# Decoder layer on one core: fixed order on ScalarE and VectorE through the first block of weights, first granule in quarters, other order of the first transfers

## The chip, the core and the metric

The kernel runs on one core of a Trainium2 chip. The metric is the device time of one execution in microseconds (us). The core has TensorE (PE in the rows; its weight loads are PEld), VectorE (DVE), ScalarE (ACT), GpSimd (POOL) and SyncE (SP, which here only issues transfers), each with an instruction stream of its own that runs in order, and 16 DMA engines. They wait for each other by semaphores.

## What is computed

One decoder layer on 256 tokens of width 2048, all in float32: an RMSNorm, one wide projection into nine parts, an attention branch and a gated MLP branch, and a gated merge.

```
h = rms_norm(x, norm_g)                      # (256, 2048)
q, k, v, z_a, u_b, v_b, z_b, g_a, g_b = split(h @ w_in)
q, k = rms_norm(q, q_norm_g), rms_norm(k, k_norm_g)   # per head
y_a = (attention(q, k, v) * silu(z_a)) @ w_proj_a
sgu = spatial_gating(gelu(u_b), gelu(v_b), sgu_norm_g, w_s, b_s)
y_b = (sgu * silu(z_b)) @ w_proj_b
out = x + (sigmoid(g_a) * y_a + sigmoid(g_b) * y_b) @ w_out
```

The first block of columns, q, is what this case is about: it is multiplied before the norm of x is known, and scaled by it afterwards.

## The kernel before

**Granules.** All weights are read once, as 120 granules of 128 x 2048 float32 (1 MB each). `schedule()` lists them: 8 granules for q, 8 each for k, v, za, vb, ub and zb, then the gates and projections, then the output. A granule `i` of q holds four blocks of 512 columns, of two k tiles (128 rows of the contraction) by two halves of the q columns, in the order 12, 11, 22, 21 (first digit: the k tile; second: the column half).

**Three products.** Every operand is split in two rounded parts: a high half, which ScalarE makes by a cast to fp32r (L120), and a low half, which VectorE makes by subtracting it (L121). `halve` does both, `split(i, pieces)` does it for the weights of granule `i` (`raw` gives `wh` and `wl`), `split_x(kp)` for two k tiles of the transposed x. A product is then three matmuls of 128 x 128 by 512 columns (`three`, L275), so a plain granule takes 24 of them (`direct`). From k on, granules 4, 5, 6 and 7 of a block are plain, and 0 to 3 go by a scheme of seven products (`seven`), for which VectorE makes sums `t` of the weights (L138 to L141) that are split too (`th`, `tl`; the remaining weights are `whp`, `wlp`); such a granule takes 21.

**The first block.** For q the x that is multiplied is not yet normalised. `split_x` multiplies each k tile of x by `norm_g` on ScalarE (L191, 256 columns), casts two of them into `xuh` (L194) and VectorE subtracts to give `xul` (L195). Beside this, `stats` squares the two halves of the plain x (`xnat`, L229), `rsqrt` makes `rstd` of the sums on VectorE and GpSimd (L224, L225), and `stats_row` turns it into a row `R` by two transposes on TensorE (`ps_R`, L235) and a copy. They stand in TensorE's program between the fourth and the fifth granule. From `R` on, `normalise`, `halves_x`, `forms` and `halves_f` make the normalised x for all later blocks (L243, L249, L257 to L260, L267). When q is done it is scaled by `rstd` while it leaves PSUM (L613), and its heads are squared (L339) and scaled (L351).

**What sets the order.** SP issues the transfers in the order of its program: `vec` (the norm vectors, 26 columns), x by k tiles (`load_x`), and the granules (`load`, `load_piece`); a granule's transfer waits for its buffer (four `raw` buffers). On the other engines a scheduler orders instructions when the program is built. Under `tc.manual_schedule` the instructions of ScalarE and VectorE keep among themselves the order in which the code stands; here this covers L581 to L585, the splits of the first four pairs of k tiles and of the first two granules. The loop that follows splits granule `i + 2` and, for `i` under 4, the pair `i + 4` of k tiles, loads granule `i + 3`, and multiplies granule `i`.

Of the kernel before, what the change touches and what calls it, by code (L numbers as in the profile page):

```python
# [64 lines left out]
def hybrid_layer_kernel(  # L65
# [29 lines left out]
    def f(ap):  # L95
        return ap.bitcast(F32)
# [58 lines left out]
    vec = const.tile([P, NVEC], F32, name="vec")  # L155
# [3 lines left out]
    def load_x(p0, p1):  # L159
        nc.sync.dma_start(xt[p0 // 8][:, p0 % 8:(p1 - 1) % 8 + 1, :],  # L160
                          xT[:, NVEC + p0 * S:NVEC + p1 * S].rearrange("p (k t) -> p k t", t=S))

    new_raw(0)
    nc.sync.dma_start(vec, xT[:, 0:NVEC])
    load_x(0, 2)
    load_piece(0, 0, 512)
    load_piece(0, 512, 1024)
    load_x(2, 4)
    load_piece(0, 1024, WORDS)
    load_x(4, 8)  # L170
    load(1, pieces=2)
    load_x(8, 12)
    load(2, pieces=2)
# [14 lines left out]
    def split_x(kp):  # L188
        i, a = kp // 4, 2 * (kp % 4)
        for j in range(2):  # L190
            nc.scalar.activation(xt[i][:, a + j, :], xt[i][:, a + j, :], AF.Copy,  # L191
                                 scale=vec[:, 2 * kp + j:2 * kp + j + 1])
        src = xt[i][:, a:a + 2, :]
        nc.scalar.copy(xu_h[i][:, a:a + 2, :], src)  # L194
        nc.vector.tensor_tensor(xu_l[i][:, a:a + 2, :], src, f(xu_h[i][:, a:a + 2, :]), op=ALU.subtract)  # L195
# [23 lines left out]
    R = const.tile([P, S], F32, name="R")  # L219
# [59 lines left out]
    def direct(L, hs, ls, i, kp, start, stop):  # L279

        t, a = kp // 4, 2 * (kp % 4)
        for c in range(4):
            r, col = c // 2, c % 2
            for kh in range(2):
                hi = hs[t][:, a + kh, r * P:(r + 1) * P]
                lo = ls[t][:, a + kh, r * P:(r + 1) * P]
                o = BLK[f"{kh + 1}{col + 1}"] * B
                three(L[c], hi, lo, wh[i][:, o:o + B], wl[i][:, o:o + B], start and kh == 0, stop and kh == 1,
                      first=(i == 0))
# [291 lines left out]
    with tc.manual_schedule(engines={mybir.EngineType.Activation, mybir.EngineType.DVE}):  # L581
        for kp in range(4):
            split_x(kp)
            if kp < 2:
                split(kp, 2)  # L585
    E, L = [0, 2, 4, 3], [1, 5, 6, 7]
    e = None
    for i, (kind, name, c, kp, n) in enumerate(G):
        if i < 4:
            split_x(i + 4)  # L590
        load(i + 3, pieces=2 if i < 2 else 1)
        split(i + 2)
# [116 lines left out]
```

## Time and profile before

| | |
|---|---|
| median of three runs | 692.8 us (692.78 to 693.59) |
| profiled execution | 692.96 us |
| its span, first to last instruction | 691.2 us |
| TensorE busy | 664.2 us (96%), 3018 matmuls |
| VectorE busy | 553.6 us (80%) |
| ScalarE busy | 388.9 us (56%) |
| DMA | 135.31 MB, mean 196 GB/s |

The share of busy time is a mean over stages that differ, so it doesn't tell by itself what a change is worth. A row of the timeline has the start, the duration, the engine, the line in the code, the operation, what it writes and reads by the names of the program, the number of instructions in the row, and, in brackets, how long the engine was idle ahead of it and what ended that wait. Matmuls overlap: the distance between two starts is what one costs, not the duration. All times are counted from the start of the span.

### The profile page before, as it was taken

How to read it: one execution, taken by the hardware profiler on the slowest of the kernel's cores; microseconds unless marked ns; L12 is line 12 of the kernel's file. 1: busy time of each engine (PE TensorE's matmuls, PEld its weight loads, DVE VectorE, ACT ScalarE, POOL GpSimd, SP SyncE). 2: the span in 40 equal slices, each digit the busy share in tenths (PEclk: the TensorE clock that was granted, in tenths of full speed). 3: DMA queues.
4: the chain of work that ended last, by engine and by line, in shares of the span. 5: the costliest groups of instructions: out<-in, count | busy, mean ns of one | idle time of the engine just before them, and what ended most of it. 6: DMA issues, size and time to landing. Idle time of an engine off the chain costs nothing.

```text
span 691.2 us, 7699 instructions
## 1 busy us (share of the span) xinstructions
PE 664.2 (96%) x3018; PEld 547.6 (79%) x3018; DVE 553.6 (80%) x498; ACT 388.9 (56%) x453; POOL 37.0 (5%) x28
## 2 busy tenths in 40 slices
PE   2799999999999999999999999999999999999997
PEld 0588778888889888788877888888888888888886
DVE  0669789989999899999898998878968886754451
ACT  2959757955785477564745744563554455333330
POOL 1000400500000006200000000000000000000000
PEclk9999999999999999999999999999999999999999
DMA  8863436563274454525734834854563576856610
GB/s 315 332 212 119 167 128 252 183 241 132 116 300 166 162 195 146 228 114 183 290 136 167 320 122 183 303 183 156 220 245 142 201 263 213 267 189 227 235 47 30
DMA packets 22211, 135.31 MB, mean 196 GB/s; under 512 B 2592, under 2 KB 2976, under 8 KB 7200
## 3 DMA queue, kind: packets, MB, share of 16 engines
q1 hardware_dynamic: 21024, 132.73, 51.9%
q10 hardware_dynamic: 1152, 2.10, 1.1%
q8 instruction: 23, 0.38, 0.2%
q14 instruction: 12, 0.10, 0.0%
HBM read 132.72 MB, written 2.10 MB: 195 GB/s over the span
## 4 chain that ended last, share of the span: by engine, by line
PE 85%; DVE 8%; DMA 2%; issue 2%; ACT 2%; POOL 1%; SPq 0%; DVEq 0%; ACTq 0%
PE acc_g L275 14%; PE y L275 13%; PE acc_out L275 13%; PE seven_g L275 5%; PE acc_ub L275 4%; PE acc_v L275 4%; PE acc_q L275 4%; PE acc_za L275 4%; PE acc_vb L275 4%; PE acc_zb L275 4%; DMA xt<-in_xT 2%; PE acc_k L275 2%; DVE wl L121 2%; PE seven_v L275 2%; PE seven_ub L275 2%
## 5 line engine op out<-in xcount | busy, mean ns | idle before, releaser
L121 DVE TENSOR_TENSOR wl<-raw,wh 128x2048 fp32r<-128x2048 f32 (+1 forms) x82 | 182.7, 2236 | 65.6 <-ACT wh L120 65.3
L120 ACT CAST wh<-raw 128x2048 fp32r<-128x2048 f32 (+1 forms) x82 | 153.0, 1870 | 106.5 <-PE acc_out L275 42.2
L120 ACT CAST th<-t 128x2048 fp32r<-128x2048 f32 x40 | 76.5, 1912 | 105.6 <-DVE t L141 105.5
L121 DVE TENSOR_TENSOR tl<-t,th 128x2048 fp32r<-128x2048 f32 x40 | 92.0, 2301 | 28.2 <-ACT th L120 27.6
L275 PE MATMUL acc_out<-wh,mT 128*128 128x512 f32 x256 | 79.0, 390 | 0.0
L120 ACT CAST whp<-raw 128x1536 fp32r<-128x1536 f32 x40 | 59.1, 1480 | 34.5 <-DMA raw<-in_w 16.2
L121 DVE TENSOR_TENSOR wlp<-raw,whp 128x1536 fp32r<-128x1536 f32 x40 | 70.1, 1752 | 0.0
L275 PEld LDWEIGHTS acc_out<-wh,mT 128*128 128x128 f32 x256 | 47.9, 188 | 9.9
L275 PE MATMUL acc_g<-wh,xh 128*128 128x512 f32 x128 | 49.8, 389 | 0.0
L275 PE MATMUL acc_out<-wl,mT 128*128 128x512 f32 x128 | 49.8, 389 | 0.0
L275 PE MATMUL acc_g<-wh,xl 128*128 128x512 f32 x128 | 49.7, 389 | 0.0
L138 DVE TENSOR_TENSOR t<-raw 128x1024 f32<-128x1024 f32 x40 | 48.8, 1221 | 0.6
L275 PE MATMUL acc_g<-wl,xh 128*128 128x512 f32 x128 | 48.8, 389 | 0.0
L275 PE MATMUL acc_q<-wh,xuh 128*128 128x512 f32 x64 | 26.0, 407 | 16.9 <-ACT wh L120 16.9
L225 POOL TENSOR_TENSOR rs<-ms,mhalf 128x4 f32<-128x4 f32 x12 | 29.8, 2506 | 126.0 <-DVE ms L224 126.0
L275 PEld LDWEIGHTS acc_q<-wh,xuh 128*128 128x128 f32 x64 | 12.6, 196 | 20.2 <-ACT wh L120 17.8
L275 PEld LDWEIGHTS acc_g<-wl,xh 128*128 128x128 f32 x128 | 24.0, 188 | 5.2
L275 PEld LDWEIGHTS acc_g<-wh,xl 128*128 128x128 f32 x128 | 24.0, 188 | 5.1
L140 DVE TENSOR_TENSOR t<-t,raw 128x512 f32<-128x512 f32 x40 | 27.8, 694 | 0.3
L275 PEld LDWEIGHTS acc_out<-wl,mT 128*128 128x128 f32 x128 | 24.0, 188 | 4.9
L275 PEld LDWEIGHTS acc_g<-wh,xh 128*128 128x128 f32 x128 | 24.0, 188 | 4.9
L141 DVE TENSOR_TENSOR t<-t,raw 128x512 f32<-128x512 f32 x40 | 27.4, 686 | 0.3
(452 smaller groups left out, 1447.4 us busy)
## 6 DMA issues: line engine op xcount, KB each, us to landing
raw<-in_w SPq DMA_DIRECT2D x115, 1024.0 KB, 4.9
raw<-in_w SPq DMA_DIRECT2D x9, 512.0 KB, 8.6
xnat<-in_x SPq DMA_DIRECT2D x2, 1024.0 KB, 12.0
xres<-in_x ACTq DMA_DIRECT2D x8, 256.0 KB, 5.3
out<-xres SPq DMA_DIRECT2D x7, 256.0 KB, 4.5
xt<-in_xT SPq DMA_DIRECT2D x3, 512.0 KB, 9.2
xt<-in_xT SPq DMA_DIRECT2D x2, 256.0 KB, 4.1
raw<-in_w SPq DMA_DIRECT2D x2, 256.0 KB, 5.4
```

The lines of the kernel that those rows point to most:

```text
L120: nc.scalar.copy(h, r)
L121: nc.vector.tensor_tensor(l, r, f(h), op=ALU.subtract)
L138: nc.vector.tensor_tensor(two, r[:, B:3 * B].rearrange("p (a n) -> p a n", a=2), r[:, None, 0:B].to_broadcast([P, 2, B]), op=ALU.add)
L140: nc.vector.tensor_tensor(t[:, 2 * B:3 * B], t[:, 0:B], r[:, 2 * B:3 * B], op=ALU.add)
L141: nc.vector.tensor_tensor(t[:, 3 * B:], t[:, 2 * B:3 * B], r[:, 3 * B:], op=ALU.add)
L225: nc.gpsimd.tensor_tensor(dst, ms[:, :n], mhalf[:, :n], op=ALU.pow)
L275: nc.tensor.matmul(acc, a, b, start=(start and n == 0), stop=(stop and n == 2))
```

## The change

The tile `vec` becomes `xv`, which also takes the first k tile of x; its first transfer brings both. The first granule comes in pieces of 512, 512 and 1024 columns, the second k tile between them, and the other transfers at the start alternate in another order: `raw3` is issued whole ahead of the last piece of x and of `xnat`, and `raw4` whole behind them. `R` takes the place of the first k tile in `xv`. `split_x` can take one k tile alone, and the first granule is split by quarters, each beside the k tile that it is multiplied with; the second granule is split in quarters too, the third in halves. `direct` multiplies the first granule quarter by quarter. The manual order of ScalarE and VectorE goes on through the loop until the eighth granule, and in the loop the split of the weights stands ahead of that of x.

```diff
--- before.py
+++ after.py
@@ -152,7 +152,9 @@
         return ap.rearrange("p (h d) -> p h d", d=P)
 
 
-    vec = const.tile([P, NVEC], F32, name="vec")
+
+    xv = const.tile([P, NVEC + S], F32, name="xv")
+    vec = xv[:, 0:NVEC]
     xt = [slot(F32, f"xt{i}").rearrange("p (k t) -> p k t", t=S) for i in range(2)]
     xu_h, xu_l = [], []
 
@@ -161,16 +163,17 @@
                           xT[:, NVEC + p0 * S:NVEC + p1 * S].rearrange("p (k t) -> p k t", t=S))
 
     new_raw(0)
-    nc.sync.dma_start(vec, xT[:, 0:NVEC])
-    load_x(0, 2)
-    load_piece(0, 0, 512)
-    load_piece(0, 512, 1024)
+    nc.sync.dma_start(xv, xT[:, 0:NVEC + S])
+    load_piece(0, 0, B)
+    load_piece(0, B, 2 * B)
+    load_x(1, 2)
+    load_piece(0, 2 * B, WORDS)
     load_x(2, 4)
-    load_piece(0, 1024, WORDS)
+    load(1, pieces=2)
     load_x(4, 8)
-    load(1, pieces=2)
+    load(2, pieces=2)
     load_x(8, 12)
-    load(2, pieces=2)
+    load(3)
     load_x(12, 16)
     xn = [slot(F32, f"xnat{m}") for m in range(2)]
     for m in range(2):
@@ -185,14 +188,15 @@
     for _ in range(8):
         nc.tensor.matmul(ps_w, warm[:, 0:P], warm, start=True, stop=True)
 
-    def split_x(kp):
+    def split_x(kp, js=None):
         i, a = kp // 4, 2 * (kp % 4)
-        for j in range(2):
-            nc.scalar.activation(xt[i][:, a + j, :], xt[i][:, a + j, :], AF.Copy,
-                                 scale=vec[:, 2 * kp + j:2 * kp + j + 1])
-        src = xt[i][:, a:a + 2, :]
-        nc.scalar.copy(xu_h[i][:, a:a + 2, :], src)
-        nc.vector.tensor_tensor(xu_l[i][:, a:a + 2, :], src, f(xu_h[i][:, a:a + 2, :]), op=ALU.subtract)
+        for j in js or range(2):
+            src = xv[:, NVEC:] if kp + j == 0 else xt[i][:, a + j, :]
+            nc.scalar.activation(xt[i][:, a + j, :], src, AF.Copy, scale=vec[:, 2 * kp + j:2 * kp + j + 1])
+        sl = slice(a + js[0], a + js[0] + 1) if js else slice(a, a + 2)
+        src = xt[i][:, sl, :]
+        nc.scalar.copy(xu_h[i][:, sl, :], src)
+        nc.vector.tensor_tensor(xu_l[i][:, sl, :], src, f(xu_h[i][:, sl, :]), op=ALU.subtract)
 
     ident = const.tile([P, P], F32, name="ident")
     make_identity(nc, ident)
@@ -216,7 +220,7 @@
         nc.sync.dma_start(gain, bass.AP(tensor=sg.tensor, offset=sg.offset, ap=[[0, P], [1, P]]))
 
     rstd = const.tile([P, 2], F32, name="rstd")
-    R = const.tile([P, S], F32, name="R")
+    R = xv[:, NVEC:]
     ssum = const.tile([P, 2], F32, name="ssum")
 
     def rsqrt(dst, src, n, count):
@@ -279,14 +283,16 @@
     def direct(L, hs, ls, i, kp, start, stop):
 
         t, a = kp // 4, 2 * (kp % 4)
-        for c in range(4):
+        order = [(c, kh) for c in range(4) for kh in range(2)]
+        if i == 0:
+            order = [(c, kh) for kh in range(2) for col in (1, 0) for c in (col, 2 + col)]
+        for c, kh in order:
             r, col = c // 2, c % 2
-            for kh in range(2):
-                hi = hs[t][:, a + kh, r * P:(r + 1) * P]
-                lo = ls[t][:, a + kh, r * P:(r + 1) * P]
-                o = BLK[f"{kh + 1}{col + 1}"] * B
-                three(L[c], hi, lo, wh[i][:, o:o + B], wl[i][:, o:o + B], start and kh == 0, stop and kh == 1,
-                      first=(i == 0))
+            hi = hs[t][:, a + kh, r * P:(r + 1) * P]
+            lo = ls[t][:, a + kh, r * P:(r + 1) * P]
+            o = BLK[f"{kh + 1}{col + 1}"] * B
+            three(L[c], hi, lo, wh[i][:, o:o + B], wl[i][:, o:o + B], start and kh == 0, stop and kh == 1,
+                  first=(i == 0))
 
     def seven(E, L, i, kp, first, last, started):
 
@@ -578,18 +584,28 @@
     for c in range(4):
         at(first["out", 0] + 4 * c - 2, load_res, c)
 
-    with tc.manual_schedule(engines={mybir.EngineType.Activation, mybir.EngineType.DVE}):
-        for kp in range(4):
-            split_x(kp)
-            if kp < 2:
-                split(kp, 2)
+    ordered = ExitStack()
+    ordered.enter_context(tc.manual_schedule(engines={mybir.EngineType.Activation, mybir.EngineType.DVE}))
+    split_x(0, [0])
+    split(0, 4, [0])
+    split(0, 4, [1])
+    split_x(0, [1])
+    split(0, 4, [2])
+    split(0, 4, [3])
+    for kp in range(1, 4):
+        split_x(kp)
+        if kp < 2:
+            split(kp, 4)
     E, L = [0, 2, 4, 3], [1, 5, 6, 7]
     e = None
     for i, (kind, name, c, kp, n) in enumerate(G):
+        if i == 8:
+            ordered.close()
+        if i:
+            load(i + 3)
+        split(i + 2, 2 if i == 0 else 1)
         if i < 4:
             split_x(i + 4)
-        load(i + 3, pieces=2 if i < 2 else 1)
-        split(i + 2)
         plain = i < 8
         if kind == "quad":
             if n == 0:
```

The sequence of ScalarE at its start; `xt0` and `xt1` hold the k tiles 0 to 7 and 8 to 15 of x, `wh0` is the high half of the first granule. Before:

```order
L191 ACT_TABLE_LOAD
L191 ACTIVATE xt0_74<-xt0_74,vec_73 128x256 x2
L191 ACTIVATE xt1_75<-xt1_75,vec_73 128x256 x8
L194 CAST xuh0_96<-xt0_74 128x512
L120 CAST wh0_133<-raw0_76 128x1024 x2
L191 ACTIVATE xt0_74<-xt0_74,vec_73 128x256 x2
L194 CAST xuh1_98<-xt1_75 128x512
L194 CAST xuh0_96<-xt0_74 128x512
L120 CAST wh1_143<-raw1_84 128x1024 x2
```

After:

```order
L195 ACT_TABLE_LOAD
L195 ACTIVATE xt0_74<-xv_73 128x256
L198 CAST xuh0_98<-xt0_74 128x256
L120 CAST wh0_133<-raw0_76 128x512 x2
L195 ACTIVATE xt0_74<-xt0_74,xv_73 128x256
L198 CAST xuh0_98<-xt0_74 128x256
L120 CAST wh0_133<-raw0_76 128x512 x2
L195 ACTIVATE xt0_74<-xt0_74,xv_73 128x256 x2
L198 CAST xuh0_98<-xt0_74 128x512
L120 CAST wh1_150<-raw1_83 128x512 x4
```

The eight scalings of `xt1` have gone from in front of the first casts, and the first cast of weights stands behind one scaling and one cast; each of the first pieces is half as large.

The sequence of ScalarE around the squares of `xnat` (L229, then L233), on which `rstd` waits. Before:

```order
L120 CAST wh3_204<-raw3_162 128x2048
L194 CAST xuh1_98<-xt1_75 128x512
L229 ACTIVATE xnat0_92,ssum_126<-xnat0_92 128x2048
L120 CAST wh4_238<-raw4_201 128x2048
L229 ACTIVATE xnat1_93,ssum_126<-xnat1_93 128x2048
L194 CAST xuh1_98<-xt1_75 128x512
L120 CAST wh5_277<-raw5_236 128x2048
L120 CAST wh6_311<-raw6_275 128x2048
```

After:

```order
L120 CAST wh3_208<-raw3_91 128x2048
L195 ACTIVATE xt1_75<-xt1_75,xv_73 128x256 x2
L198 CAST xuh1_100<-xt1_75 128x512
L120 CAST wh4_242<-raw4_206 128x2048
L195 ACTIVATE xt1_75<-xt1_75,xv_73 128x256 x2
L198 CAST xuh1_100<-xt1_75 128x512
L233 ACTIVATE xnat0_94,ssum_127<-xnat0_94 128x2048
L233 ACTIVATE xnat1_95,ssum_127<-xnat1_95 128x2048
L120 CAST wh5_281<-raw5_240 128x2048
L195 ACTIVATE xt1_75<-xt1_75,xv_73 128x256 x2
```

Before, the first square stood ahead of `wh4`; now both stand behind it and behind the sixth and seventh pair of k tiles.

The sequence of TensorE in the third and fourth granule of k's block (`th10`, `tl10`, `th11`, `tl11` are the split sums of these two, `Fh` a form of x). Before:

```order
L275 MATMUL acc_k0_0_470<-whp11_504,xl0_411 128x512
L275 MATMUL acc_k0_0_470<-whp11_504,xh0_410 128x512
L275 MATMUL acc_k0_0_470<-wlp11_505,xh0_410 128x512
L275 MATMUL acc_k0_1_471<-whp11_504,Fl_415 128x512
L275 MATMUL acc_k0_1_471<-whp11_504,Fh_414 128x512
L275 MATMUL acc_k0_1_471<-wlp11_505,Fh_414 128x512
L275 MATMUL acc_k0_2_472<-th11_508,xl0_411 128x512
L275 MATMUL acc_k0_2_472<-th11_508,xh0_410 128x512
L275 MATMUL acc_k0_2_472<-tl11_509,xh0_410 128x512
L275 MATMUL seven_k0_0_582<-whp11_504,xl0_411 128x512
```

After:

```order
L279 MATMUL acc_k0_2_481<-tl10_476,xh0_418 128x512
L279 MATMUL seven_k0_1_592<-tl10_476,Fh_422 128x512
L279 MATMUL seven_k0_2_593<-tl10_476,Fh_422 128x512
L279 MATMUL seven_k0_3_594<-tl10_476,Fh_422 128x512
L279 MATMUL acc_k0_2_481<-th11_517,xl0_419 128x512
L279 MATMUL acc_k0_2_481<-th11_517,xh0_418 128x512
L279 MATMUL seven_k0_1_592<-th11_517,Fl_423 128x512
L279 MATMUL seven_k0_1_592<-th11_517,Fh_422 128x512
L279 MATMUL seven_k0_2_593<-th11_517,Fl_423 128x512
L279 MATMUL seven_k0_2_593<-th11_517,Fh_422 128x512
L279 MATMUL acc_k0_2_481<-tl11_518,xh0_418 128x512
```

The row with `tl11` was the ninth of the fourth granule and the 78th of the block; now the products of the third granule with `tl10` and six with `th11` stand ahead of it, and it is the 85th.

## Rows read from the trace of the kernel before

**Rows 1.** The page's slices: TensorE's busy tenths in 40 equal slices of the span.

```profile
PE   2799999999999999999999999999999999999997
```

**Rows 2.** Timeline of ScalarE, start of the span: start, duration, what, [idle before <-releaser].

```profile
14.72 1.70 ACT L191 ACTIVATE xt<-xt,vec 128x256 f32<-128x256 f32 x4 [8.60 <-DMA xt<-in_xT]
18.55 1.70 ACT L191 ACTIVATE xt<-xt,vec 128x256 f32<-128x256 f32 x4 [2.13 <-DMA xt<-in_xT]
...
20.67 1.99 ACT L120 CAST wh<-raw 128x1024 fp32r<-128x1024 f32 x2
...
27.11 1.90 ACT L120 CAST wh<-raw 128x2048 fp32r<-128x2048 f32 x1
28.91 0.61 ACT L194 CAST xuh<-xt 128x512 fp32r<-128x512 f32 x1
```

**Rows 3.** Timeline of TensorE, the block of q.

```profile
21.76 0.80 PE L275 MATMUL acc_q<-wh,xuh 128*128 128x512 f32 x1 [16.92 <-ACT wh L120]
...
26.17 0.63 PE L275 MATMUL acc_q<-wh,xuh 128*128 128x512 f32 x1
26.60 0.52 PE L275 MATMUL acc_q<-wh,xul 128*128 128x512 f32 x1
...
46.24 0.38 PE L235 MATMUL ps_R<-ident,rstd 128*128 128x128 f32 x2
```

**Rows 4.** DMA issues of the first 2 us: KB each, median us to landing.

```profile
xt<-in_xT SPq DMA_DIRECT2D x1, 256.0 KB, 2.6
...
vec<-in_xT SPq DMA_DIRECT2D x1, 13.0 KB, 1.9
```

**Rows 5.** Timeline of GpSimd, the powers that make the norms.

```profile
39.89 1.21 POOL L225 TENSOR_TENSOR rstd<-ms,mhalf 128x2 f32<-128x2 f32 x1 [36.78 <-DVE ms L224]
76.31 6.93 POOL L225 TENSOR_TENSOR rs<-ms,mhalf 128x4 f32<-128x4 f32 x4 [35.20 <-DVE ms L224]
```

**Rows 6.** Window 10 to 12 us: busy by engine, clock, DMA share, GB/s (last).

```profile
10.00:12.00 2.00, 0.00 (x0) 0.00 (x0) 0.00 (x0) 0.00 (x0) 0.00 (x0) 1.00 1.03 420
```

**Rows 7.** Timeline of ScalarE, the first square and the reading of its sum.

```profile
33.60 1.91 ACT L229 ACTIVATE xnat<-xnat 128x2048 f32<-128x2048 f32 x1
35.42 0.18 ACT L229 ACTIVATION_READ_ACCUMULATOR xnat<-xnat 128x1 f32 x1
```

**Rows 8.** Windows behind two waits of TensorE: third column from the end is PEclk.

```profile
89.00:90.00 1.00, 1.00 (x4) 0.81 (x3) 1.00 (x2) 1.00 (x5) 0.00 (x0) 0.50 0.00 0
360.00:365.00 5.00, 5.00 (x23) 4.02 (x23) 5.00 (x3) 4.36 (x3) 0.00 (x0) 1.00 0.51 210
```

**Rows 9.** Timeline of TensorE, a wait in the block of the gates.

```profile
359.73 0.50 PE L275 MATMUL acc_g<-th,xl 128*128 128x512 f32 x1 [1.72 <-ACT th L120]
```

**Rows 10.** Timeline of TensorE, the block of k.

```profile
68.23 0.39 PE L275 MATMUL acc_k<-wh,xl 128*128 128x512 f32 x1
...
87.65 0.50 PE L275 MATMUL acc_k<-tl,xh 128*128 128x512 f32 x1 [1.59 <-DVE tl L121]
...
92.33 0.40 PE L275 MATMUL acc_k<-wh,xl 128*128 128x512 f32 x1
```

**Rows 11.** Timeline of VectorE, from the normalisation to the sums of k.

```profile
50.36 4.49 DVE L243 TENSOR_TENSOR xt<-xt,R 128x2048 f32<-128x2048 f32 x2
54.77 2.29 DVE L121 TENSOR_TENSOR wl<-raw,wh 128x2048 fp32r<-128x2048 f32 x1
...
59.17 0.69 DVE L257 TENSOR_TENSOR F<-xt 128x512 f32<-128x512 f32 x1
...
70.39 1.22 DVE L138 TENSOR_TENSOR t<-raw 128x1024 f32<-128x1024 f32 x1
71.52 1.75 DVE L121 TENSOR_TENSOR wlp<-raw,whp 128x1536 fp32r<-128x1536 f32 x1
```

**Rows 12.** Timeline of ScalarE, eviction of q and the last of its squares.

```profile
66.78 2.42 ACT L613 ACTIVATE q<-acc_q,rstd 128x512 f32<-128x512 f32 x4
...
73.66 0.20 ACT L339 ACTIVATION_READ_ACCUMULATOR junk<-q 128x1 f32 x1
```


## The prediction

> **What bounds the kernel now.** I read the page's slices first. The row of TensorE is full from the second slice to the last but one [rows 1]: apart from its first 20 us, TensorE sets the end, and a gain has to come from TensorE starting earlier or waiting less. Second, the timeline of ScalarE shows what keeps it from starting. After the first two k tiles ScalarE takes two groups of four scalings of `xt` that wait 8.60 us and 2.13 us for transfers; by the order of the program they belong to `xt1`, that is to the fifth to eighth granule. Only behind them come `xuh0` and the cast of `wh0` at 20.67 [rows 2]. Third, the timeline of TensorE: the first matmul of the block of q starts at 21.76 after a wait of 16.92 us for that cast [rows 3].
>
> **The start itself.** With the new order ScalarE needs, ahead of the first matmul, the transfer `xv`, one scaling, one cast of 256 columns and one of 512. `xv` is issued first; the nearest rows are `vec` (13 KB, 1.9 us) and the first `xt` (256 KB, 2.6 us) [rows 4], so it lands some 2.7 to 3.4 us into the span, and the first quarter of the weights two to four us later. A scaling is 0.43 (four in 1.70), a cast of 512 columns 0.61 [rows 2]; a cast of 256 isn't in the trace, it lies between nothing and that 0.61, and I take 0.35, since it would be nearer to the scaling of the same size. The first matmul then starts between 4 and 10; I take 7, some 14.8 us earlier. **This isn't the gain**, since TensorE soon meets something that moved less.
>
> **The cap: the transposes `ps_R` in front of the fifth granule.** They stand in TensorE's order ahead of its matmuls and need `rstd`, which needs the squares of both `xnat`. Before, `rstd` was there at 41.1 (39.89 + 1.21) [rows 5], and TensorE came to `ps_R` only at 46.24 [rows 3]. After, ScalarE's order there is the cast of `wh4`, scalings and cast of `xt1`, square, square, and `raw4` stands behind both `xnat` on the queue of SP. The DMA engines are the clock: they move 420 GB/s [rows 6]. At 18.55 a scaling was let go by the last piece of `xT` [rows 2]; up to that piece the queue held 5.26 MB (`vec` 13 KB, `xT` 2.10, three granules of 1.05). After, up to the end of `raw4`, it holds `xv` and the rest of `xT` 2.11 MB, five granules 5.24, `xnat` 2.10, `gain` 0.07: 9.52 MB. The other 4.26 MB take 10.1 us, so `raw4` lands at **28.7**. ScalarE is idle by then: up to `raw3` it is 5.78 MB, so 19.8, and the cast of it and one more split of x end 3.2 later. From 28.7: cast `wh4` 1.8 (27.11 to 28.91), two scalings and a cast 1.35 [rows 2], two squares of 1.9 (33.60 to the next instruction behind 35.42) [rows 7], `ms` with its hops, which I put at 0.25, GpSimd 1.21 [rows 5]. That is 28.7 + 1.8 + 1.35 + 3.8 + 0.25 + 1.2 = **37.1**. TensorE is there first: the 96 matmuls from 46.24 to 68.23 take 0.23 each [rows 3, 10], at the low clock 0.43 (26.17 to 26.60) [rows 3]; one granule of 24 at 0.43 is 10.3, three at 0.23 are 16.5, so from 7 it has done four at 33.8. A start 3 us later than I take costs nothing. `ps_R` moves from 46.24 to 37.1: **-9.1 us**.
>
> **What the wait costs behind it.** In the trace of before, after its long wait, TensorE starts a matmul every 0.43 us until 26.60: eleven from 21.76 in 4.84 us [rows 3], where 0.23 each would be 2.5. [...] Here it idles some 3.3 us ahead of `ps_R`, and I charge the same: **+2.3 us**. [...]
>
> **Where the block of k gains.** Before, this block begins at 68.23, and its 78th matmul, the first with `tl11`, starts at 87.65 [rows 10]. 77 at 0.23 are 17.6 us, so 1.8 were lost. The next 13 take until 92.33, 4.7 us where 3.0 would do: 1.7 more at the low clock. `th11` stood behind scalings of q, which waited for GpSimd. After, one scaling stands ahead of `th10`, three ahead of `th11`, and TensorE takes the first product with `tl11` in the 85th place. Does VectorE keep up? The block of q ends at T = 37.1 + 22.0 + 2.3 = 61.4. VectorE's chain starts with `R`: ScalarE has a cast `wh5` (1.8) and the last split of x (1.35) behind the squares, then the copy `R`, about 0.4, and `wh6` 1.8, so `wl6` starts at 41.0. From there to the end of `t11`: seven subtractions of 2.2 (2.29, overlapping by 0.08), two normalisations 4.4, two `wlp` of 1.7, four forms of 0.6, two sums t of 2.3 (1.13 + 2 x 0.6), `ms` 0.5, a wait of 1.9 for `xh1`: 15.4 + 4.4 + 3.4 + 2.4 + 4.6 + 0.5 + 1.9 = 32.6, so 73.6 [rows 11]. On ScalarE, q is evicted and squared in 7.1 us (66.78 to 73.86) [rows 12], to 68.5; `ms` is at 70.4 on VectorE, GpSimd adds 0.25 + 1.73 (6.93 / 4) [rows 5], one scaling 0.3, `th10` 1.8 to 74.5, three scalings 0.9, `th11` 1.8 to 77.2, `tl11` 2.2 to 79.4. TensorE wants it at T + 84 x 0.23 = 80.7, 1.3 us later. So the loss goes: **-3.5 us**.
>
> **What costs nothing.** Quarters in the first two granules are four more casts on ScalarE and four more subtractions on VectorE. Two casts of 1024 columns take 1.99 [rows 2], four of 512 some 2.1 to 2.4: 0.1 to 0.4 a granule, ahead of ScalarE's idle time from 23.0 to 28.7, which hides it; without that cover it would be up to 0.8. [...] `R` in the place of the first k tile orders its copy behind the scalings, which are on the same engine. `raw3` and `raw4` in one transfer instead of two change no byte count.
>
> **Sum.** -9.1 + 2.3 - 3.5 = -10.3 us. The profiled execution took 692.96 us (span 691.2), the median is 692.8; 692.96 - 10.3 = 682.7, against the median 682.5. I forecast **682.6 us**.
>
> **The rivals.** (1) *VectorE takes over.* Its margin at `tl11` is 1.3 us, since its normalisation moves from 50.36 [rows 11] to 43.2, 7 us, and TensorE 10. If `R` or `th11` is 2 us late, the stall of before stays, 682.6 + 3.5 = 686.1, and two such give 689.6. For it: in those rows VectorE goes from one instruction to the next without idle time. Against: the new order of TensorE puts its products later. Chance 0.24. (2) *The clock stays up behind `ps_R`, or `raw4` lands earlier*: 682.6 - 2.3 = 680.3, with both 679. For it the wait at 359.73, against it those at 21.76 and 87.65. 0.13. (3) *Slower than before*: TensorE, now 3 us nearer to VectorE, waits for `tl` in granule after granule of k, v and za, each time with the low clock behind it. One such wait costs 3.5, as at 87.65; it decides from the third on (682.6 + 3 x 3.5 = 693.1), and with four the time is 696.6. Against: each wait of TensorE lets VectorE get ahead, so the second is less likely than the first. 0.05. (4) *It doesn't do what it says*: the first pieces land no sooner and the front still starts near 20. Then `ps_R` is 24.5 us behind it as before, near 44.5: 1.7 us, and at most the 3.5 of k, 687.6 to 692.8. ScalarE's order is fixed in the program, so only the transfers could do it, and the new order puts the needed ones first. 0.04.
>
> **How the numbers follow.** My own case has 0.54, between 680.8 and 685 (`raw4` an us off, half the slow stretch). The range, 679.0 to 688.5, takes in rival 2 and the first stall of rival 1 and leaves out the rest. A measurement of this kernel tells about 0.2%, 1.4 us, from no change. Faster by more: 0.54 + 0.24 + 0.13 and a part of rival 4, 0.92; within it 0.03; slower 0.05.
>
> **What would show it.** Right: the first matmul between 4 and 10; ScalarE idle ahead of `wh4`, which starts near 28.7; TensorE idle ahead of `ps_R`, which starts near 37; matmuls 0.43 apart behind it; the block of k beginning near 61.4; no wait for `tl11`. Wrong: TensorE still in its fourth granule at 37, `ps_R` before 35 or after 39, or waits for `tl` or `wl` behind 61.

## The result, and the profile after

The changed kernel takes **687.2 us** (median; runs from 687.0 to 687.55) against 692.9 for the kernel before on the same chip: a ratio of 0.992, 95% interval 0.9908 to 0.9933. It is faster, by 5.7 us (0.8%, clear of the noise) where 10.3 were forecast; 687.2 lies in the range of 679.0 to 688.5, in its upper quarter, and outside the 680.8 to 685 of the prediction's own case. The profiled execution took 687.05, with a span of 685.3.

The page's slices are read first again, against [rows 1]: TensorE's busy tenths.

```profile
PE   8789999999999999999989999999999999999997
```

The empty first slice is gone; there is a dent in the third, and that is the wait ahead of `ps_R`. The timeline of ScalarE answers to [rows 2] (start, duration, what, [idle before <-releaser]):

```profile
3.07 0.51 ACT L195 ACTIVATE xt<-xv 128x256 f32<-128x256 f32 x1 [0.99 <-DMA xv<-in_xT]
...
28.36 1.91 ACT L120 CAST wh<-raw 128x2048 fp32r<-128x2048 f32 x1 [5.58 <-DMA raw<-in_w]
...
38.67 0.37 ACT L240 COPY xv<-ps_R 128x256 f32<-128x256 f32 x1
```

The copy of `R` (the last row) stood at 48.02 in the kernel before:

```profile
48.02 0.36 ACT L236 COPY R<-ps_R 128x256 f32<-128x256 f32 x1
```

GpSimd makes `rstd` in 0.71 us, where [rows 5] had 1.21:

```profile
35.81 0.71 POOL L229 TENSOR_TENSOR rstd<-ms,mhalf 128x2 f32<-128x2 f32 x1 [32.71 <-DVE ms L228]
```

And the timeline of TensorE answers to [rows 3] and [rows 10]: first matmul, `ps_R`, the first matmuls of the blocks of k, v and g.

```profile
6.46 0.50 PE L279 MATMUL acc_q<-wh,xuh 128*128 128x512 f32 x1 [1.61 <-ACT wh L120]
...
36.57 0.69 PE L239 MATMUL ps_R<-ident,rstd 128*128 128x128 f32 x2 [6.82 <-POOL rstd L229]
36.91 0.78 PE L279 MATMUL acc_q<-wh,xul 128*128 128x512 f32 x1
...
39.60 0.40 PE L279 MATMUL acc_q<-wh,xul 128*128 128x512 f32 x1
...
60.04 0.39 PE L279 MATMUL acc_k<-wh,xl 128*128 128x512 f32 x1
...
102.41 0.39 PE L279 MATMUL acc_v<-wh,xl 128*128 128x512 f32 x1
...
334.52 0.39 PE L279 MATMUL acc_g<-wh,xl 128*128 128x512 f32 x1
```

Set beside the kernel before, the blocks start earlier by:

| block | before | after | earlier by | length before | length after |
|---|---|---|---|---|---|
| `ps_R` | 46.2 | 36.6 | 9.7 | | |
| k | 68.2 | 60.0 | 8.2 | 44.5 | 42.4 |
| v | 112.8 | 102.4 | 10.4 | 42.8 | 45.3 |
| za | 155.6 | 147.7 | 7.9 | 48.0 | 48.0 |
| vb | 203.6 | 195.7 | 7.9 | 48.8 | 48.9 |
| ub | 252.4 | 244.6 | 7.8 | 43.3 | 44.8 |
| zb | 295.7 | 289.4 | 6.3 | 44.5 | 45.1 |
| g | 340.2 | 334.5 | 5.7 | | |

So the forecast gain was there: 10.4 us at the start of v, by the working 10.3. **4.7 us of it were given back behind that point**: 2.5 in v, 0.1 in vb, 1.5 in ub, 0.6 in zb (they are called the 4.6 us below: 10.3 forecast less 5.7 measured). From g on the two kernels run alike. The waits view of TensorE in the changed kernel says by what (us in total, times, longest):

```profile
PE ps_R L239 <- POOL rstd L229: 6.8, 1, 6.8
PE acc_g L279 <- ACT th L120: 3.1, 2, 1.7
...
PE acc_v L279 <- ACT th L120: 1.3, 2, 0.7
...
PE acc_ub L279 <- ACT th L120: 0.8, 1, 0.8
PE acc_k L279 <- ACT th L120: 0.8, 1, 0.8
PE acc_ub L279 <- DVE tl L121: 0.7, 1, 0.7
PE acc_zb L279 <- ACT th L120: 0.3, 1, 0.3
```

The waits in g stand in the kernel before too [rows 9]. The other rows below the first are short waits for `th` and `tl`, the halves of the sums in the scheme of seven products. In v, ub and zb the kernel before had none.

### The profile page after: what moved, and what is told of

It is laid out like the page before. It is cut to its first block, busy times and chain, and to the rows that moved or that the text cites. A ratio compares the mean times of both kernels' runs of the same rounds, so it can differ in the third digit from the quotient of the medians.

```text
span 685.3 us, 7695 instructions
## 1 busy us (share of the span) xinstructions
PE 664.1 (97%) x3018; PEld 545.4 (80%) x3018; DVE 554.3 (81%) x504; ACT 390.4 (57%) x459; POOL 31.9 (5%) x28
## 4 chain that ended last, share of the span: by engine, by line
PE 69%; DVE 15%; issue 5%; ACT 4%; DMA 4%; SPq 1%; POOL 0%; DVEq 0%; ACTq 0%
PE acc_g L279 14%; PE y L279 13%; PE acc_out L279 13%; PE seven_g L279 5%; PE acc_za L279 4%; PE acc_vb L279 4%; DMA raw<-in_w 4%; DVE wl L121 3%; ACT th L120 2%; PE acc_zb L279 2%; DVE wlp L121 2%; PE acc_v L279 2%; DVE t L138 2%; DVE tl L121 2%; PE acc_ub L279 2%
## 5 line engine op out<-in xcount | busy, mean ns | idle before, releaser
L121 DVE TENSOR_TENSOR wl<-raw,wh 128x2048 fp32r<-128x2048 f32 (+2 forms) x87 | 183.2, 2116 | 68.0 <-ACT wh L120 67.8
L120 ACT CAST wh<-raw 128x2048 fp32r<-128x2048 f32 (+2 forms) x87 | 153.7, 1774 | 103.8 <-PE acc_out L279 45.7
L279 PEld LDWEIGHTS acc_out<-wh,mT 128*128 128x128 f32 x256 | 47.9, 188 | 9.8
L279 PE MATMUL acc_g<-wl,xh 128*128 128x512 f32 x128 | 48.8, 389 | 0.0
L229 POOL TENSOR_TENSOR rs<-ms,mhalf 128x4 f32<-128x4 f32 x12 | 25.2, 2119 | 128.4 <-DVE ms L228 128.4
L279 PE MATMUL acc_q<-wl,xuh 128*128 128x512 f32 x64 | 25.7, 401 | 0.3 <-DVE wl L121 0.2
```

The costliest lines, as they stand in the source:

```text
L120: nc.scalar.copy(h, r)
L121: nc.vector.tensor_tensor(l, r, f(h), op=ALU.subtract)
L229: nc.gpsimd.tensor_tensor(dst, ms[:, :n], mhalf[:, :n], op=ALU.pow)
L279: nc.tensor.matmul(acc, a, b, start=(start and n == 0), stop=(stop and n == 2))
```

## The experiments

Three theories were set against each other for the 4.6 us. **A**: VectorE's whole work from `R` on paces the kernel, so the end follows the start of that chain. **B**: the places that the scheduler gave ScalarE's casts in v (a scaling of k that waits for GpSimd stands ahead of a cast `th`). **C**, formed after the first four runs: VectorE's work inside v to ub is too long for what TensorE leaves it, and what is saved before v doesn't count. Beside these, the parts of the change were tried one by one. All ratios are to the kernel before. "Third" or "fourth granule" of a block means its place in the order of multiplication (4, 5, 0, 1, 6, 2, 3, 7).

### What the start needs: parts of the change alone

**The fixed order alone**, in the kernel before:

```diff
-    with tc.manual_schedule(engines={mybir.EngineType.Activation, mybir.EngineType.DVE}):
-        for kp in range(4):
+    ordered = ExitStack()
+    ordered.enter_context(tc.manual_schedule(engines={mybir.EngineType.Activation, mybir.EngineType.DVE}))
+    for kp in range(4):
...
-        if i < 4:
-            split_x(i + 4)
+        if i == 8:
+            ordered.close()
         load(i + 3, pieces=2 if i < 2 else 1)
         split(i + 2)
+        if i < 4:
+            split_x(i + 4)
```

> The kernel before, its transfers and halves left as they are, with the fixed order on ScalarE and VectorE carried on through the block of q alone. The first matmul then waits for two k tiles and half a granule and starts some 3 us later than the 6.46 of the changed kernel. If the start has slack because ps_R waits for rstd (6.8 us of wait in the changed kernel), ps_R comes within 1 us of 36.6 and the time is 687.2, within 0.9 of the changed kernel. If the new transfers and quarters carry part of the gain, ps_R comes 3 us later or more and the time is 690 or above.

Measured: 688.37 us, ratio 0.9931 (0.9917 to 0.9946). The first matmul starts at 8.69, and the wait ahead of `ps_R` is 1.91 in place of 6.82:

```profile
37.62 0.43 PE L235 MATMUL ps_R<-ident,rstd 128*128 128x128 f32 x2 [1.91 <-POOL rstd L225]
```

The order alone brings 4.6 of the 5.7 us. Whether the other 1.2 us belong to the change isn't shown: the two intervals overlap, and `ps_R`, 1.05 later here, moves as much between kernels that are alike up to it (36.57 in the changed kernel, 37.71 in the run with the scaling behind the cast below). The next run tries the halves by themselves.

**Halves in place of quarters**, in the changed kernel:

```diff
-        if i == 0:
-            order = [(c, kh) for kh in range(2) for col in (1, 0) for c in (col, 2 + col)]
...
-    split_x(0, [0])
-    split(0, 4, [0])
...
-            split(kp, 4)
+    for kp in range(4):
+        split_x(kp)
+        if kp < 2:
+            split(kp, 2)
...
-        split(i + 2, 2 if i == 0 else 1)
+        split(i + 2)
```

> The changed kernel with the first two granules in halves again and the first granule's products in the old order; transfers and the fixed order as in the changed kernel. If the start has slack ahead of ps_R: the first matmul 1 to 3 us later than 6.46, ps_R within 1 us of 36.6 and the same time, 687.2. If the quarters carry gain: 688.5 or more.

Measured: 687.15, ratio 0.992 (0.9903 to 0.9937), against 687.2 with quarters. The first matmul is 2.5 us later, and the wait ahead of `ps_R` takes it up:

```profile
8.94 0.80 PE L279 MATMUL acc_q<-wh,xuh 128*128 128x512 f32 x1 [4.09 <-ACT wh L120]
...
36.61 0.69 PE L239 MATMUL ps_R<-ident,rstd 128*128 128x128 f32 x2 [3.77 <-POOL rstd L229]
```

The quarters and the new order of products are worth nothing that can be measured. What the fixed order alone lacks belongs to the transfers, if to a part of the change at all; that wasn't tried by itself.

**Without the fixed order**, the new transfers and quarters alone (the order ended ahead of the loop over the granules):

```diff
     E, L = [0, 2, 4, 3], [1, 5, 6, 7]
+    ordered.close()
...
-        if i == 8:
-            ordered.close()
```

> The changed kernel with the fixed order ended behind the first two granules, as in the kernel before: new transfers and quarters alone. The scheduler then puts eight scalings of xt1 ahead of the first cast again; the last of them needs the last piece of xT, which now stands behind 6.3 MB in place of 5.26, 2.5 us later. If the fixed order is what frees TensorE's start: the first matmul near 24, ps_R near 48 and a time between 692 and 695. If transfers and quarters carry the gain: ps_R near 37 and 687 to 688.

Measured: 693.51, ratio 1.001 (1.0001 to 1.002). ScalarE's timeline has the eight scalings back ahead of the first cast. The second four of them wait for a transfer until 20.31, and TensorE starts behind them (a row of each engine):

```profile
20.31 1.70 ACT L195 ACTIVATE xt<-xt,xv 128x256 f32<-128x256 f32 x4 [2.06 <-DMA xt<-in_xT]
```

```profile
22.88 0.79 PE L279 MATMUL acc_q<-wh,xuh 128*128 128x512 f32 x1 [18.03 <-ACT wh L120]
```

The fixed order is what frees the start. (`ps_R` came at 46.1, not at 48: TensorE made its four granules in 23.2 us where [rows 3] had 24.5.)

### What holds TensorE ahead of `ps_R`

**The squares one granule earlier**, into the 5.58 us in which ScalarE waits for `raw4`:

```diff
-    at(i0 + 2, stats)
+    at(i0 + 1, stats)
```

> The changed kernel with the two squares for rstd put one granule earlier in ScalarE's order, ahead of the cast of wh4, into ScalarE's idle time of 5.6 us that waits for raw4. rstd then comes near 30 in place of 36.5, ps_R waits little or nothing (TensorE's fourth granule ends near 29.8), and the copy R comes near 35 in place of 38.67, since the cast wh5 and a split of x stay ahead of it. Theory A, the end follows the chain that starts at R: 3.6 us less, 683.6. If TensorE's wait at ps_R is what counts: 6 to 7 us less, 680.5. If waits in v and ub absorb an earlier start: 687.2.

Measured: **683.56**, ratio 0.9865 (0.985 to 0.9879), the 683.6 of theory A, and 3.6 us better than the changed kernel. ScalarE's and TensorE's timelines:

```profile
35.14 0.37 ACT L240 COPY xv<-ps_R 128x256 f32<-128x256 f32 x1
```

```profile
29.27 0.38 PE L239 MATMUL ps_R<-ident,rstd 128*128 128x128 f32 x2
30.27 0.50 PE L279 MATMUL acc_q<-wh,xul 128*128 128x512 f32 x1 [0.61 <-ACT wh L120]
...
32.60 0.53 PE L279 MATMUL acc_q<-wl,xuh 128*128 128x512 f32 x1 [1.59 <-DVE wl L121]
```

So the cap of the prediction is shown: with `rstd` earlier, `ps_R` starts 7.3 us earlier and waits for nothing. Of the 7.3, 4.4 arrive at the block of k (55.6), since now `wh4` and `wl4`, which need `raw4`, are late, with slow matmuls behind (0.43 apart from 33.35 to 35.91). The waits in v, ub and zb are all still there (v lasts 44.9, ub 44.7, zb 45.4): moving everything forward by some 4 us doesn't change what is lost behind v. `R` is copied 3.5 us earlier (35.14 against 38.67), v starts 3.5 us earlier and the end comes 3.6 us earlier: that is theory A's forecast.

### Where the 4.6 us went

**2.2 us less for VectorE ahead of v**: the subtraction for one half of `xl` is left out, in the block of q (lines of the edit that only keep the tile apart are not shown).

```diff
         nc.scalar.copy(xh[i], xt[i])
+        if i == 1:
+            xl[i] = xu_l[i]
+            return
         nc.vector.tensor_tensor(xl[i], xt[i], f(xh[i]), op=ALU.subtract)
```

> The changed kernel without the subtraction that forms the low half of the second eight normalised k tiles (2.2 us of VectorE right behind the first normalisation; the low half of the unscaled tiles stands in its place), the order of everything else on ScalarE and VectorE unchanged. Theory A, VectorE's work from R on sets the end: 2.2 us less, 685.0. If TensorE's own chain or waits for ScalarE set it: no change, 687.2.

Measured: 687.61, ratio 0.992 (0.9903 to 0.9936): nothing gained. In this profile v starts at 102.3 and lasts 45.3, with the same three waits, at the same places within 0.2 us. That takes nothing from theory A, because the time of this subtraction wasn't on the chain. VectorE's timeline in the changed kernel, and then without it:

```profile
47.35 2.29 DVE L253 TENSOR_TENSOR xl<-xt,xh 128x2048 fp32r<-128x2048 f32 x1 [1.98 <-ACT xh L252]
49.56 2.29 DVE L121 TENSOR_TENSOR wl<-raw,wh 128x2048 fp32r<-128x2048 f32 x1
```

```profile
49.47 2.29 DVE L121 TENSOR_TENSOR wl<-raw,wh 128x2048 fp32r<-128x2048 f32 x1 [3.78 <-ACT wh L120]
```

VectorE's next instruction waits for ScalarE's cast `wh` and starts where it did before, so the 2.2 us became idle time. What does set the start of v shows when the copy of `R` is taken as zero (all in us; the last three columns are distances):

| kernel | copy of `R` | start of v | `R` to k | `R` to v | `R` to g |
|---|---|---|---|---|---|
| before | 48.0 | 112.8 | 20.2 | 64.7 | 292.1 |
| new transfers, without the fixed order | 47.9 | 111.4 | 20.2 | 63.5 | 292.0 |
| changed | 38.7 | 102.4 | 21.4 | 63.7 | 295.8 |
| fixed order alone | 39.7 | 103.5 | 20.0 | 63.8 | 295.7 |
| early squares | 35.1 | 98.9 | 20.5 | 63.7 | 295.7 |
| early squares, normalisation split (below) | 36.2 | 99.9 | 18.4 | 63.7 | 295.7 |
| subtraction left out (this run) | 39.0 | 102.3 | 22.1 | 63.3 | 295.4 |

In all twelve traces with the fixed order, v starts 63.3 to 63.8 us behind the copy of `R`, while the block of k starts anywhere from 18.4 to 22.7 behind it; the waits of TensorE in k take up the difference. So up to v the chain of ScalarE and VectorE that goes through this copy paces the kernel, as theory A has it, and a TensorE that reaches k sooner gains nothing.

**2.2 us less for VectorE in v**: one subtraction `wl` left out, ahead of the final sums of k. In the changed kernel it starts at 101.91, half a us ahead of v.

```diff
+                if i != first["v", 0] + 1:
+                    wl[i] = wpool.tile([P, WORDS], F32R, tag="wl", bufs=3, name=f"wl{i}")
+            if i == first["v", 0] + 1:
+                nc.scalar.copy(wh[i], r)
+                wl[i] = wh[i]
+                return
```

> The changed kernel without one subtraction wl (2.2 us of VectorE just ahead of the final sums of k; the granule of v that uses it takes the high half in place of the low one); the order through the block of v is otherwise unchanged. Theory C, VectorE's list between the start of v and its second cast th is too long: the block of v takes 43.5 or less in place of 45.3, with no or one wait in place of three; what follows then waits in ub as before, so 685.5. Theory B, the scaling that waits for GpSimd or the release of a buffer by TensorE makes these waits: 45.3 and 687.2.

Measured: 684.97, ratio 0.9897 (0.9881 to 0.9914): 2.2 us less than the changed kernel, as much as VectorE was spared. The windows view by block, VectorE alone (window, its length, busy us and instructions, PEclk, DMA share, GB/s), shows where: v and the sum of the four blocks v, za, vb, ub, of the kernel before and of the changed one, and v, ub and the sum of this one.

```profile
112.80:155.60 42.80, 40.25 (x38) 1.00 0.54 197
...
sum 182.90, DVE 174.41; mean DVE 43.60
```

```profile
102.40:147.70 45.30, 39.88 (x37) 1.00 0.51 187
...
sum 187.00, DVE 174.72; mean DVE 43.68
```

```profile
102.50:146.60 44.10, 38.60 (x36) 1.00 0.53 196
...
243.40:286.80 43.40, 42.49 (x54) 1.00 0.48 183
sum 184.30, DVE 172.49; mean DVE 43.12
```

From the start of v to the end of ub VectorE works the same 174 us before and after, but the stretch has grown from 182.9 to 187.0. VectorE's idle time grew from 8.5 to 12.3 us, most of it in v (from 2.6 to 5.4). Take 2.2 us of its work out at the start of v, and the stretch shrinks by 2.7: v by 1.2, and ub by 1.4, a hundred microseconds on, where both waits are gone.

In v VectorE's instructions keep their order, and its rows stand some 2.3 us earlier (the `tl` of v's fourth granule at 119.86, not 122.16): there its work is on the path, which theories A and C both have. The gain in ub can't be put down to the work alone. The scheduler chose another order in this kernel, which the expectation took to be as before at least through v: on ScalarE in v, za and vb, on VectorE in za, vb and ub. In ub VectorE now makes the `ms` of vb's norms ahead of the sums they stood behind, and no longer waits 0.98 us for GpSimd, as in the changed kernel (first row), but 0.16 (second):

```profile
261.90 1.93 DVE L365 SCALAR_TENSOR_TENSOR vb_c<-vb_c,rs,gain 128x128 f32<-128x128 f32 x7 [0.98 <-POOL rs L229]
```

```profile
259.04 2.19 DVE L370 SCALAR_TENSOR_TENSOR vb_c<-vb_c,rs,gain 128x128 f32<-128x128 f32 x8 [0.16 <-POOL rs L234]
```

So theory C isn't separated from an order of instructions that suits ub better.

**The scaling of k behind the cast `th`** (theory B by itself: nothing else changes place on ScalarE and VectorE). In the changed kernel the idle time of VectorE in v lies at two places, shown here by the rows of ScalarE and VectorE. The second stands in the kernel before too (2.05 us, at 145.41); at the first it had 0.39 (at 128.40). The cast at 137.36 is put down to TensorE, but the sum `t` of VectorE that it casts ends only 0.11 us ahead of it.

```profile
119.64 0.70 ACT L357 ACTIVATE k_c<-k_c,rs 128x128 f32<-128x128 f32 x2 [3.43 <-POOL rs L229]
120.24 1.89 ACT L120 CAST th<-t 128x2048 fp32r<-128x2048 f32 x1
...
137.36 1.91 ACT L120 CAST th<-t 128x2048 fp32r<-128x2048 f32 x1 [4.62 <-PE seven_v L279]
```

```profile
122.16 2.29 DVE L121 TENSOR_TENSOR tl<-t,th 128x2048 fp32r<-128x2048 f32 x1 [3.27 <-ACT th L120]
...
139.30 2.29 DVE L121 TENSOR_TENSOR tl<-t,th 128x2048 fp32r<-128x2048 f32 x1 [2.05 <-ACT th L120]
```

```diff
+            if fn is norm_qk and a[0] == "k":
+                with tc.issue_after(getattr(cast_t[i + 0], "ins", cast_t[i + 0])):
+                    fn(*a)
```

(`cast_t[i]` is ScalarE's cast `th` of v's fourth granule; the lines that keep it are not shown.)

> The changed kernel, with the sixteen scalings of k on ScalarE put behind the cast th of v's fourth granule, so that this cast no longer stands behind a scaling that waits 3.43 us for GpSimd; nothing else changes place on ScalarE and VectorE. Theory B, the order that the scheduler chose in v is what gave back 4.6 us: 682.6 to 684. Theory A, VectorE's work paces: the sums for this cast end at 118.74 and it starts at 120.24, so 1.4 us at most: 685.8. If waits further on set the end, no change: 687.2.

Measured: 687.43, ratio 0.9919 (0.9904 to 0.9934). In its profile v lasts 44.4 in place of 45.3 and VectorE's idle time there falls by 0.8 us; but `ps_R` came 1.1 us later in that execution, and the end shows no gain. From the copy of `R` to g it is 295.2 us in place of 295.8. Made again on top of the early squares:

> The changed kernel with the squares one granule earlier and k's scalings behind the cast th of v's fourth granule. Alone, the second edit shortened the block of v by 0.9 us (45.3 to 44.4), but that kernel's first part ran 1.1 us later by its profile and its time did not fall. If the 0.9 is real and stays: 682.7. If VectorE, short of time up to the end of ub, gives it back there: 683.6.

Measured: 683.19, ratio 0.986 (0.9845 to 0.9875), against 683.56 (0.985 to 0.9879) without it. The difference of 0.4 is below what these runs tell apart; from the copy of `R` to g the trace has 295.2 us, 295.7 without the edit. Theory B, as one misplaced scaling that costs all the 4.6 us, falls; by the traces the scaling is worth 0.5 to 0.7 us.

**VectorE relieved in ub by GpSimd**, the normalisation of vb moved (the edit is shortened here: `rs` stands for `X["rs", "vb", m, c]`, and the loops around it are left out):

```diff
-                    nc.vector.scalar_tensor_tensor(sl, sl, rs[:, h:h + 1], gain, op0=ALU.mult, op1=ALU.mult)
+                nc.gpsimd.tensor_tensor(t, t, rs[:, 0:4, None].to_broadcast([P, 4, P]), op=ALU.mult)
+                nc.gpsimd.tensor_tensor(t, t, gain[:, None, :].to_broadcast([P, 4, P]), op=ALU.mult)
```

> The changed kernel with the normalisation of vb taken from VectorE (16 instructions of 128x128, some 4.5 us in the block of ub) and done by eight multiplications on GpSimd; the order of everything else on TensorE, ScalarE and VectorE is unchanged. Theory C: in the block of ub VectorE has more to do between the block's start and the last tl than TensorE leaves it (it runs without a gap from 263.74 to 281.02), so both waits of TensorE in ub (0.71 and 0.84, with their restart 1.9) go, the block takes 43.0 in place of 44.8 and the time is 685.4. Theory B, waits come from the places the scheduler gave ScalarE's casts: block 44.8, time 687.2. If GpSimd is too slow or slows VectorE down, mix waits at the start of zb: 688 or more.

Measured: 694.92, ratio 1.0039 (1.0026 to 1.0052), slower than the kernel before; the block of ub takes 52.7. VectorE's rows while GpSimd works, and the longest of TensorE's waits:

```profile
271.50 1.52 DVE L140 TENSOR_TENSOR t<-t,raw 128x512 f32<-128x512 f32 x1
...
280.83 3.37 DVE L121 TENSOR_TENSOR tl<-t,th 128x2048 fp32r<-128x2048 f32 x1
```

```profile
279.52 0.50 PE L279 MATMUL acc_ub<-th,xl 128*128 128x512 f32 x1 [2.69 <-ACT th L120]
```

A sum of 128x512 takes 1.52 in place of 0.69, a `tl` 3.37 in place of 2.29. VectorE lost more by this (7.5 us over the eight longer instructions that start from 265.65 to 284.12) than the 4.5 us it was spared, and TensorE stood still for it: in ub, too, VectorE is on the path. All three edits together show the same:

> The changed kernel with the squares one granule earlier, the normalisation of vb on GpSimd and k's scalings behind the cast th of v's fourth granule. If the three add up: 683.6 with the squares alone, less 1.9 in ub (if that relief works) and 0.9 in v: 680.8. If TensorE, further ahead, only waits elsewhere: 683 to 683.6.

Measured: 690.82, ratio 0.9972 (0.996 to 0.9983): the early squares' 3.6 us less what GpSimd costs in ub, which lasts 52.5 here too.

**VectorE relieved in ub by ScalarE**, on top of the early squares (shortened in the same way):

```diff
-                    nc.vector.scalar_tensor_tensor(sl, sl, rs[:, h:h + 1], gain, op0=ALU.mult, op1=ALU.mult)
+                    nc.scalar.activation(sl, sl, AF.Copy, scale=rs[:, h:h + 1])
+                nc.vector.tensor_tensor(t, t, gain[:, None, :].to_broadcast([P, 4, P]), op=ALU.mult)
```

> The changed kernel with the squares one granule earlier, and the normalisation of vb split: the scaling by rs on ScalarE (16 instructions), the product with the gain on VectorE in four instructions of 128x512 (some 2.8 us in place of 4.5). If VectorE's work in ub sets TensorE's waits there: 1.5 us less than with the squares alone, 682.1. If ScalarE's casts th come later behind scalings that wait for GpSimd: 684 to 686.

> The changed kernel with the squares early, the normalisation of vb split as in the run before, and k's scalings behind the cast th of v's fourth granule. If all add up: 681.2. If the scalings on ScalarE cost what VectorE saves: 682.7 to 684.

Measured: 684.09, ratio 0.9875 (0.9858 to 0.9892), and 683.91, ratio 0.9863 (0.984 to 0.9886): no gain over 683.56 that these runs tell apart (one of the four runs of the second took 680.97, and in both profiles `R` came 1.0 us later than in that of the early squares). Of the two waits in ub one is gone, and the other is longer. On ScalarE the scheduler now puts the copy of `seven_ub` ahead of the last `th`, and TensorE waits for the `th` behind it:

```profile
276.70 0.59 ACT L323 COPY ub_c<-seven_ub 128x512 f32<-128x512 f32 x1 [4.52 <-PE seven_ub L279]
277.18 1.90 ACT L120 CAST th<-t 128x2048 fp32r<-128x2048 f32 x1
```

```profile
279.14 0.50 PE L279 MATMUL acc_ub<-th,xl 128*128 128x512 f32 x1 [2.48 <-ACT th L120]
```

Here it is an order that costs 2.5 us, where this wait was 0.8: a wait for TensorE ahead of what TensorE waits for. So B is a real mechanism in ub with this edit; whether it took a part of the 4.6 us is taken up at the end of the next section.

The best of these kernels differ from the changed one by the early squares: 683.56, and 683.19 with the scalings of k moved too, against 687.2 and 692.9.

## Why the prediction was right, and where not

**What bounds it: right for the kernel before.** TensorE sets its end, and ScalarE's hoisted scalings kept it from starting. Without the fixed order they are back, and the time is that of the kernel before. In the changed kernel TensorE sets less of it: its share of the chain that ended last is 69% on the page, before 85%, and VectorE's 15%, before 8%.

**The start: right, and so is that it isn't the gain.** 6.46 against the forecast 7. A start at 8.94 (the halves) costs nothing; the wait ahead of `ps_R` shrinks by as much.

**The cap: right**, and shown by the early squares. The row of `wh4` has 28.36 where `raw4` was put at 28.7; `ps_R` started at 36.57 against 37.1. Most of that half microsecond is GpSimd's 0.71 against 1.21. The wait was 6.8, not 3.3 us, because the first granules ran at 0.23 a matmul almost from the first on and were done at 29.75, not at 33.8. This cost nothing, since the wait's end was not TensorE's to set.

**The slow clock behind the wait: it came, and cost less than was charged.** The granted clock behind `ps_R` reads 0.50 and then 1.00 (windows: PE, PEld, DVE, ACT, POOL busy, then PEclk):

```profile
36.90:39.60 2.70, 2.70 (x8) 2.15 (x7) 2.26 (x2) 2.67 (x6) 0.00 (x0) 0.50 0.13 55
39.60:41.00 1.40, 1.40 (x8) 1.14 (x7) 0.76 (x3) 1.25 (x1) 0.00 (x0) 1.00 0.56 70
122.00:125.00 3.00, 2.60 (x10) 1.87 (x11) 2.84 (x2) 3.00 (x3) 2.38 (x4) 1.00 0.78 325
```

Six matmuls from 36.91 to 39.60 took 2.7 us where 0.23 each make 1.4: 1.3 us, not 2.3. The 9.7 us by which `ps_R` came earlier outweighed it.

**The block of k: the sum right by luck, the terms not.** k began at 60.0, not 61.4, and was to lose its whole stall of 3.5. `tl11` ended at 79.34 (forecast 79.4), but TensorE, 1.4 us ahead of the forecast, was there by then: its matmul started 0.05 us later, at 79.39, 0.49 behind the one ahead of it where 0.23 is the pace. The margin of 1.3 us was gone, with no wait booked. At 94.07 came a wait of 0.75 for the `th` of the seventh granule, and the block got only 2.1 us shorter. The two errors of 1.4 cancel: v was to begin 10.3 us earlier and began 10.4 earlier.

**The sum: here it failed.** The step was to take VectorE's margin at one place, `tl11` in k, to book the stall there as saved (-3.5), and to carry the sum unchanged to the end. Measured in the same terms, k began 8.2 us earlier (forecast 6.8: -9.1 + 2.3), and from there to g TensorE took 274.5 us in place of 271.9, which is 2.5 longer and not 3.5 shorter. In place of TensorE the chain that goes through the copy of `R` sets the pace up to v: `R` came 9.35 us earlier, and v follows it at 63.7 us. Neither the slow clock behind `ps_R` nor the stall of k is a term of that chain. Behind v, from the start of v to the end of ub, VectorE has the same 174 us of work in a stretch that left it 8.5 us idle before. That this idle time leaves nothing over at the places that count could have been read off the kernel before, in the rows of ScalarE and TensorE in ub; the third row is the same cast in the changed kernel:

```profile
284.73 1.91 ACT L120 CAST th<-t 128x2048 fp32r<-128x2048 f32 x1 [3.17 <-DVE t L141]
```

```profile
286.70 0.49 PE L275 MATMUL acc_ub<-th,xl 128*128 128x512 f32 x1
```

```profile
279.08 1.91 ACT L120 CAST th<-t 128x2048 fp32r<-128x2048 f32 x1 [3.18 <-DVE t L141]
```

The cast ends at 286.64, and the matmul that needs it starts 0.06 us later: no wait is booked, and no margin is left. A TensorE that comes earlier there waits, unless the casts come earlier by as much; they came 5.7 us earlier (279.08 against 284.73), and 5.7 us is what is left of the gain at g.

**Rival 1 is what happened**, in mechanism though not in its condition or price. It had VectorE take over at `tl11` in k if `R` or `th11` were 2 us late, at 3.5 us a stall with the slow clock behind it. `R` wasn't late (38.67, about as worked out); TensorE came early. Behind k the waits came in v, ub and zb, six of them, 0.2 to 0.84 us each; no slow clock stood behind those in v (1.00 in the last window above, and from 139 to 142 too), and they sum to 3.4. Each costs some 0.26 more than is booked, since a wait counts only from the end of a matmul (0.39 us), which in a row costs 0.23, and the next step is 0.34; with that they come to 4.9, near the 4.6 that the three blocks lost. The time of the rival with one stall, 686.1, is nearer than the forecast; it had a chance of 0.24. The prediction's own sign of being wrong, waits for `tl` behind 61, was there too: 0.21 us in v and 0.71 in ub.

**Left open**: why the way from `R` to g is 3.7 us longer in the changed kernel (295.8 against 292.1), for the same work of VectorE. What differs is the order that the scheduler chose from k on. The run without the fixed order has the old one there, on all engines, and 292.0. But the old order isn't free of the limit: in that run v begins 1.4 us earlier than in the kernel before, and lasts 44.0 us in place of 42.8, with two waits of TensorE for VectorE that the kernel before hasn't; this is the first:

```profile
114.56 0.50 PE L279 MATMUL acc_v<-wh,xl 128*128 128x512 f32 x1 [0.28 <-DVE k_h L326]
```

The old order from k on under the new start wasn't tried, so that the new order costs the 3.7 us is likely and not shown. VectorE's idle time in v, which doubled, grew at one place: ahead of the `tl` of v's fourth granule, behind the scaling of k that waits for GpSimd, it is 3.27 us, where the kernel before had 0.39. Moving that scaling gave 0.8 us of the 2.8 back. The 0.6 us in zb were not looked into.

## What to carry to other kernels

Where a start is moved, the gain ends at the first place behind it at which another engine arrives just in time, and "just in time" shows in the kernel before as no wait at all (in ub 0.06 us from the end of the cast to its matmul): compare the end of each producer with the start of its consumer, not only the waits. Work taken off a busy engine counts only if no wait for another engine stands right behind it: 2.2 us ahead of a wait for ScalarE gave nothing, 2.2 us on the chain gave 2.2. To see which event sets a later one, take the distance between the two over all traces: from `R` to v it was the same within 0.5 us, while the start of k between them moved by 4.2. And a wait on one side can be filled with what the other side waits for: the squares, put into 5.6 us of idle ScalarE, were worth 3.6 us for one changed number.

## What the runs showed of the hardware

- While GpSimd multiplied (the normalisation of vb on GpSimd, from 270.75 to 285.35), VectorE's sums and subtractions took longer: 1.52 us in place of 0.69 for 128x512, 3.37 in place of 2.29 for 128x2048. GpSimd's own products of 128x512 took 1.5 to 3.3 us where VectorE's sums of that size take 0.69.
- The length of a wait alone doesn't tell TensorE's clock behind it: behind 1.59 us of idle time in the block of q (early squares, at 32.60) matmuls came 0.43 apart and the clock from 33 to 36 is 0.50, behind 1.72 us in the block of g it stayed at 1.00 [rows 8, 9].
- The pace behind the very first matmul varied between kernels whose first instructions are alike: 0.23 us from 7.52 on in the changed kernel, 0.43 up to 9.07 with the early squares, where the window from 5.9 to 9 has a granted clock of 1.00. In the kernel before the clock from 21.76 to 26.60 reads 1.00 too, so the 0.43 that the prediction puts down to the low clock there [rows 3] came at a granted 1.00.
- A power on GpSimd for 128x2 took 0.71 us here and 1.21 in the kernel before [rows 5].
